# Differential attention in a two-layer decoder trunk: the second run of projection products goes ahead of the output transposes

## The chip, the cores and the metric

The kernel runs on one core of one Trainium2 chip. The metric is the device time of one execution in microseconds (us). Each kernel is timed in several runs, and the median is compared. A single further execution is recorded by the hardware profiler; its times are the ones in the rows below.

## What is computed

The reference is a trunk of two pre-norm layers for 256 tokens of width 1024. Layer 0 mixes tokens with a causal Conformer convolution, layer 1 with causal differential attention. Behind each mixer come a hierarchical mixture of experts and a gated embedding; a final norm ends the trunk. The part that matters here is the attention of layer 1, with 8 heads, two score maps for each head and blocks of 128 queries:

```
qkv = h @ w_qkv                       # (256, 3 * 1024)
q, k = partial_rope(q), partial_rope(k)
for blk in range(2):                  # kend = 128, then 256 keys
    s = einsum("bqhcd,bkhcd->bhcqk", qb, kb) * scale
    a = softmax(where(mask, s, neg))
    wgt = a[:, :, 0] - lam * a[:, :, 1]
    outs.append(einsum("bhqk,bkhd->bqhd", wgt, vb))
o = rms_norm(concat(outs), subln_g) * (1 - lam_init)
return o @ w_o
```

## The kernel before

The order of the instructions on each engine is the order in which the program writes them; every engine works through its own list in that order, and waits in it are resolved by semaphores. Weights stream through a ring of 16 tiles (`wslot`), loaded by SyncE as tiles come free. A product with f32 accuracy is made of three matmuls (L433 to L435): the high halves of both factors, then each low half with the other's high half. So each weight tile is first split: ScalarE writes the high half (L190) and VectorE or, for one of four parts, GpSimd the low half (L191), in `split_part`.

The attention runs over 16 units. Unit n is one head and one block of 128 queries: `units = [(s, hh, qb) for s in range(4) for qb in range(2) for hh in range(2)]`, so four units share a group s of two heads. At n = 4, 8 and 12 `heads(n // 4)` transposes the next group's queries and keys (L1650), and ScalarE evicts them to `qkT` (L1653). Then, in each unit:

- `scores(n)`: score matmuls (L1669); VectorE adds the mask and takes the maximum (L1672, L1675); ScalarE takes the exponentials (L1678).
- `scale_out(n - 2)`: VectorE scales an older unit's output `o` by its norm (L1721).
- `differ(n)`: VectorE combines the two softmax maps into `w` (L1686 to L1690).
- a first pull of 6 products from a generator. In units 0 to 11 this is `projections()`, the products of the queries, keys and values of the next groups, which also issues the splits of later weight tiles (L190, L191), and at a tile's end ScalarE's evictions and VectorE's rotation (L1639 to L1642). In units 12 to 15 it is the output projection (`w_out`), with fewer products for each unit.
- `turn_weights(n - 1)`: transposes of `w` (L1700); ScalarE evicts them to `wT` (L1702).
- `outputs(n - 2)`: the transpose of the scaled `o` (L1727); VectorE multiplies it by the gain into `oT` (L1734). For the last group it is split into two halves, by ScalarE and VectorE.
- a second pull of 6 products.
- `values(n - 1)`: the weights times the values (L1710); ScalarE squares and copies the result (L1714, L1716), GpSimd makes its norm (L390, L391).

The transposes, the weights' transposes, the outputs and the values all take their PSUM tile from one pool of two buffers in turn:

```
def ps_b(name="psb"):
    return psum.tile([P, 512], F32, tag="b", name=name, bufs=2)
```

A unit takes three of them, in the order L1700, L1727, L1710. So the first transposes of `heads` take the buffer that L1727 wrote and L1734 must have read, the second ones that of L1710, and where no `heads` comes between, the next unit's L1700 takes the buffer of L1727.

When the 144 projection products are done, `split_heads` splits the outputs of the first groups (L1746, L1747) and the output projection starts at unit 12. After unit 15 come the routing of the second mixture of experts and its 13 steps (L1157, L1187 and others), whose weights are loaded in part by expert numbers that the routing finds.

Of the kernel before, what the change touches and what calls it, by code (L numbers as in the profile page):

```python
# [91 lines left out]
def kernel(  # L92
# [19 lines left out]
    def ps_b(name="psb"):  # L112
        return psum.tile([P, 512], F32, tag="b", name=name, bufs=2)
# [23 lines left out]
    def channels(row, k):  # L137

        return row.rearrange("p (q c) -> p q c", c=8)[:, :, 4 * k:4 * k + 4]
# [291 lines left out]
    def product(ps, h, c, wh, wl, first, last):  # L431

        nc.tensor.matmul(ps, h[:, 0, c], wh, start=first, stop=False)  # L433
        nc.tensor.matmul(ps, h[:, 0, c], wl, start=False, stop=False)  # L434
        nc.tensor.matmul(ps, h[:, 1, c], wh, start=False, stop=last)  # L435

    def warm(n):

        ps = ps_b("warm") if n else None
        for _ in range(n):  # L440
            nc.tensor.matmul(ps, ones_bf, before[:, None, :].to_broadcast([P, 4, P]), start=True, stop=True)
# [289 lines left out]
    def early(i, n0, n1):  # L731
        if n0 == 0:
            pools[i].open()
        pools[i].load(n0, n1)
# [862 lines left out]
    def attention(ap, R, end):  # L1597
# [46 lines left out]
        def heads(s, half=(0, 1)):  # L1644
            qk = qks[s]
            for hh in half:
                pt = ps_b()
                for n in range(2):
                    for tt in range(2):
                        nc.tensor.transpose(pt[:, n * T + tt * P:n * T + (tt + 1) * P],  # L1650
                                            qk[:, tt, n * 256 + hh * P:n * 256 + (hh + 1) * P], ident)
                qkT = ap.tile([P, 2, T], F32, tag="qkT", name="qkT", bufs=2)
                nc.scalar.activation(qkT.rearrange("p n t -> p (n t)"), pt, AF.Copy)  # L1653
                qkTs[2 * s + hh] = qkT
# [4 lines left out]
        def scores(n):  # L1659
            s, hh, qb = units[n]  # L1660
            qkT = qkTs[2 * s + hh]
            K = (qb + 1) * P
            psc = [ps_e() for _ in range(2)]
            mx = small.tile([P, 2], F32, tag="mx", name="mx", bufs=2)
            z = small.tile([P, 2], F32, tag="z", name="z", bufs=2)
            sc = ap.tile([P, 2, T], F32, tag="sc", name="sc", bufs=2)
            for cc in range(2):
                cs = slice(cc * HD, (cc + 1) * HD)
                nc.tensor.matmul(psc[cc][:, 0:K], qkT[cs, 0, qb * P:(qb + 1) * P], qkT[cs, 1, 0:K],  # L1669
                                 start=True, stop=True)  # L1670
            for cc in range(2):
                nc.vector.tensor_tensor_reduce(sc[:, cc, 0:K], psc[cc][:, 0:K], mask[:, T - K:],  # L1672
                                               1.0, -BIG, op0=ALU.add, op1=ALU.max,
                                               accum_out=mx[:, cc:cc + 1])
            nc.vector.tensor_scalar(mx, mx, -scale, None, op0=ALU.mult)  # L1675
            e = ap.tile([P, 2, T], F32, tag="e", name="e", bufs=2)
            for cc in (1, 0):
                nc.scalar.activation(e[:, cc, 0:K], sc[:, cc, 0:K], AF.Exp, bias=mx[:, cc:cc + 1],  # L1678
                                     scale=scale, accum_out=z[:, cc:cc + 1])
            us[n] = (e, z)  # L1680

        def differ(n):
            s, hh, qb = units[n]
            e, z = us.pop(n)
            K = (qb + 1) * P
            nc.vector.reciprocal(z, z)  # L1686
            nc.vector.tensor_mul(z[:, 1:2], z[:, 1:2], lam)
            nc.vector.tensor_scalar(e[:, 1, 0:K], e[:, 1, 0:K], z[:, 1:2], None, op0=ALU.mult)
            w = ap.tile([P, T], F32, tag="w", name="w", bufs=2)
            nc.vector.scalar_tensor_tensor(w[:, 0:K], e[:, 0, 0:K], z[:, 0:1], e[:, 1, 0:K],  # L1690
                                           op0=ALU.mult, op1=ALU.subtract)
            us[n] = w

        def turn_weights(n):
            s, hh, qb = units[n]
            w = ws[n % 2] = us.pop(n)
            K = (qb + 1) * P
            pw = ps_b()
            for kb in range(qb + 1):
                nc.tensor.transpose(pw[:, kb * P:(kb + 1) * P], w[:, kb * P:(kb + 1) * P], ident)  # L1700
            wT = ap.tile([P, T], F32, tag="wT", name="wT", bufs=2)
            nc.scalar.activation(wT[:, 0:K], pw[:, 0:K], AF.Copy)  # L1702
            us[n] = wT
# [15 lines left out]
        def scale_out(n):  # L1719
            o, ro = us[n]  # L1720
            nc.vector.tensor_scalar(o, o, ro, None, op0=ALU.mult)  # L1721
# [20 lines left out]
        def split_heads(tt, h0, h1):  # L1742
            if tt not in oTs:
                oTs[tt] = work.tile([P, 2, NH, P], F32R, tag="big", name="oTs", bufs=2)
            o = oT[tt][:, h0:h1]
            nc.scalar.activation(oTs[tt][:, 0, h0:h1], o, AF.Copy)  # L1746
            nc.vector.tensor_tensor(oTs[tt][:, 1, h0:h1], o, oTs[tt][:, 0, h0:h1].bitcast(F32), op=ALU.subtract)  # L1747
# [13 lines left out]
        def projections():  # L1761
            for g in atiles[3:]:
                yield from proj(*g)

        def outs():
            for h0, h1 in ((0, 4), (4, 6)):
                for tt in range(2):
                    yield from w_out(tt, h0, h1)
# [5 lines left out]
        def pull(f, n):  # L1774
            for _ in range(n):
                next(f, None)
# [18 lines left out]
        def residual(tt):  # L1795
            for k in range(2):
                add_half(tt, k, wo_ps[tt][k])

        def run():
            f = projections()  # L1800
            heads(0)
            for n in range(16):
                if n == 12:
                    warm(HW[0])
                if n % 4 == 0 and n:
                    heads(n // 4)
                if n == 12:
                    warm(HW[1])
                if n == 12:
                    f = outs()  # L1810
                    if not SH:
                        for tt in range(2):
                            split_heads(tt, 0, 4)
                scores(n)
                if n == 12:
                    warm(HW[2])
                if n >= 2:
                    scale_out(n - 2)
                differ(n)
                quota = QUOTA[n]  # L1820
                pull(f, quota - quota // 2)
                if n >= 1:
                    turn_weights(n - 1)
                if n >= 2:
                    outputs(n - 2)
                pull(f, quota // 2)
                if n == 11:
                    pull(f, 100)
                    if SH == 1:
                        for tt in range(2):  # L1830
                            split_heads(tt, 0, 4)
                if n >= 1:
                    values(n - 1)
                if n == 11 and SH == 2:
                    for tt in range(2):
                        split_heads(tt, 0, 4)
                if n == 13:
                    for tt in range(2):
                        split_heads(tt, 4, 6)
            def last(h):  # L1840
                wh, wl = W.parts(("wo", h // 2))
                for k in range(2):
                    product(wo_ps[1][k], oTs[1], h, channels(wh[:, h % 2], k), channels(wl[:, h % 2], k), False, h == 7)

            scale_out(14)
            pull(w_out(0, 6, 8), 5)
            early(1, 2, 3)
            residual(0)
            turn_weights(15)
            outputs(14)  # L1850
            pull(f, FT[0])
            R.rows(0, 0)
            values(15)
            scale_out(15)
            pull(f, FT[1])
            R.rows(0, 1)
            pull(f, 9)
            if LAST6 == 0:
                last(6)
            outputs(15)  # L1860
            end()
            early(1, 0, 2)
            R.logits(0, 0)
            if LAST6 == 1:
                last(6)
            R.logits(0, 1)
            R.pick(0)
            if LAST6 == 2:
                last(6)
            last(7)  # L1870
            for k in range(2):
                add_half(1, k, wo_ps[1][k])
            R.ranks(0)
            R.spots()
            R.rows(1, 0)
            W.drop(("wo", 3))
# [110 lines left out]
```

## Time and profile before

| what | us |
|---|---|
| median of 3 runs | 797.47 (794.47 to 798.09) |
| the profiled execution | 796.61 |
| its span, first to last instruction | 795.0 |
| TensorE matmul busy | 681.5 (86%) |
| VectorE busy | 385.8 (49%) |
| ScalarE busy | 297.0 (37%) |
| GpSimd busy | 115.8 (15%) |

Times in the rows are counted from the span's start. PE is TensorE's matmul, PEld its weight load, DVE VectorE, ACT ScalarE, POOL GpSimd, SP SyncE. A busy share over the whole span says little, since stages with different limits follow each other: the attention's units lie from 403 to 510 us, the second mixture of experts from 529 to 757 us. A row of a timeline gives start and duration, then the engine, line, instruction, what it writes and reads, its shape and how often it comes in a row; in brackets stands how long the engine was idle before it, and what released it. Matmuls follow each other closer than they last, because they are pipelined.

### The profile page before, as it was taken

The numbers are of one execution on the slowest core, as the hardware profiler recorded it, in microseconds if no ns is written. First come the engines' busy times: TensorE is split into PE (matmuls) and PEld (weight loads), VectorE is DVE, ScalarE is ACT, GpSimd is POOL, SyncE is SP. The second block draws the span as 40 slices with busy tenths as digits, with TensorE's granted clock in tenths as the row PEclk, the third lists the DMA queues.
The fourth block names the chain that finished last, engine by engine and source line by source line (L and its number), as shares of the span: only waits on it lengthen the run. The fifth ranks groups of instructions, "written<-read, shape, count | busy, mean of one in ns | idle before, by whom it ended". The sixth has DMA issues, their size and how long they took to land.

```text
span 795.0 us, 12692 instructions
## 1 busy us (share of the span) xinstructions
PE 681.5 (86%) x4738; PEld 444.3 (56%) x4738; DVE 385.8 (49%) x1022; ACT 297.0 (37%) x668; POOL 115.8 (15%) x191
## 2 busy tenths in 40 slices
PE   5899979889577697679999898988999999876796
PEld 4788757554234242237998696854444455523365
DVE  3599995433032320239677876562443243202174
ACT  1577733521011220018566665542222122210074
POOL 1488730000000000001023432200000000000011
PEclk9899979999899797999999999989999999998899
DMA  6991186799999999999744147857799999999941
GB/s 180 326 409 36 48 323 261 302 420 420 421 420 420 418 418 420 421 385 309 225 159 161 53 152 273 302 231 275 280 406 405 385 420 419 418 421 420 417 165 53
DMA packets 63444, 246.36 MB, mean 310 GB/s; under 512 B 7218, under 2 KB 28403, under 8 KB 43666
## 3 DMA queue, kind: packets, MB, share of 16 engines
q1 hardware_dynamic: 63234, 245.24, 79.3%
q8 instruction: 39, 0.64, 0.3%
q10 hardware_dynamic: 144, 0.26, 0.1%
q14 instruction: 27, 0.22, 0.1%
HBM read 244.43 MB, written 1.05 MB: 309 GB/s over the span
## 4 chain that ended last, share of the span: by engine, by line
PE 28%; DMA 11%; DVE 7%; ACT 6%; issue 1%; POOL 0%; POOLq 0%; ACTq 0%; SPq 0%; DVEq 0%
PE psa L1157 8%; PE psd L1187 4%; DMA wslot<-in_moe_w_up_dram 4%; DMA wslot<-in_moe_w_gate_dram 3%; DMA wslot<-in_moe_w_down_dram 2%; DMA pin<-in_p_dram 2%; PE psb L1089 2%; PE psa L433 2%; DVE wslot L191 2%; PE psa L434 2%; PE psa L435 2%; PE psd L1201 2%; ACT e L1678 1%; ACT wslot L175 1%; PE psc L434 1%
## 5 line engine op out<-in xcount | busy, mean ns | idle before, releaser
L1157 PE MATMUL psa<-wslot,hg 128*32 128x256 f32 (+2 forms) x1712 | 179.8, 474 | 54.7 <-DMA wslot<-in_moe_w_up_dram 29.5
L1157 PEld LDWEIGHTS psa<-wslot,hg 128*32 128x32 f32 (+1 forms) x1712 | 75.9, 128 | 156.0 <-issue 60.4
L1133 DVE TENSOR_REDUCE wc<-psb 32x1 f32<-32x2 f32 (+1 forms) x66 | 10.3, 156 | 197.2 <-PE psb L1128 196.6
L1187 PE MATMUL psd<-wslot,aT 128*32 128x512 f32 (+1 forms) x528 | 78.3, 596 | 6.5 <-ACT aT L1176 1.8
L1164 ACT ACTIVATE sg<-psa 128x256 f32<-128x256 f32 x20 | 7.7, 384 | 188.7 <-PE psa L1157 188.7
L1191 DVE TENSOR_TENSOR dl<-psd,dh 128x512 fp32r<-128x512 f32 x40 | 27.6, 691 | 84.8 <-ACT dh L1190 84.8
L885 PE MATMUL psa<-hT,wslot 128*128 128x256 f32 x256 | 58.6, 388 | 2.5 <-DVE hT L774 2.5
L1204 DVE TENSOR_TENSOR x<-x,psd 128x512 f32<-128x512 f32 x80 | 49.9, 681 | 16.4 <-PE psd L1201 16.4
L885 PEld LDWEIGHTS psa<-hT,wslot 128*128 128x128 f32 x256 | 49.7, 195 | 10.1 <-DVE hT L774 3.0
L1190 ACT ACTIVATE dh<-psd 128x512 fp32r<-128x512 f32 x40 | 23.8, 597 | 72.5 <-PE psd L1187 72.5
L1187 PEld LDWEIGHTS psd<-wslot,aT 128*32 128x32 f32 (+1 forms) x528 | 21.4, 115 | 52.7 <-issue 39.7
L834 DVE SCALAR_TENSOR_TENSOR chain<-vp,wT,chain 128x256 f32<-128x256 f32 x119 | 48.0, 482 | 0.2
L390 POOL TENSOR_SCALAR rstd<-ss 128x1 f32<-128x1 f32 x7 | 3.0, 425 | 292.1 <-ACT sq L397 291.2
L1094 ACT ACTIVATE hg<-psb,gains 128x256 f32<-128x256 f32 x72 | 30.1, 471 | 39.4 <-PE psb L1089 39.4
L433 PE MATMUL psa<-wslot,hTa 128*128 128x256 f32 x144 | 43.6, 302 | 0.0
L1089 PE MATMUL psb<-S,xh 128*128 128x256 f32 x144 | 38.5, 302 | 4.7 <-DVE st L1139 2.0
L434 PE MATMUL psa<-wslot,hTa 128*128 128x256 f32 x144 | 41.3, 287 | 0.0
L435 PE MATMUL psa<-wslot,hTa 128*128 128x256 f32 x144 | 41.3, 287 | 0.0
L809 ACT ACTIVATE prod<-vp,wT 128x256 f32<-128x256 f32 x83 | 35.9, 498 | 12.6 <-POOL vp L799 6.8
L814 POOL TENSOR_TENSOR part<-part,prod 128x256 f32<-128x256 f32 x51 | 35.4, 730 | 0.0
L1089 PE MATMUL psb<-S,xl 128*128 128x256 f32 x144 | 35.3, 279 | 0.0
L191 DVE TENSOR_TENSOR wslot<-wslot 128x512 fp32r<-128x512 f32 x39 | 33.4, 883 | 2.7 <-ACT wslot L190 2.7
(345 smaller groups left out, 1320.2 us busy)
## 6 DMA issues: line engine op xcount, KB each, us to landing
wslot<-in_moe_w_down_dram SPq DMA_DIRECT2D x64, 1024.0 KB
wslot<-in_moe_w_gate_dram SPq DMA_DIRECT2D x44, 1024.0 KB
wslot<-in_moe_w_up_dram SPq DMA_DIRECT2D x44, 1024.0 KB
wslot<-in_moe_w_gate_dram SPq DMA_DIRECT2D x34, 512.0 KB
wslot<-in_moe_w_up_dram SPq DMA_DIRECT2D x34, 512.0 KB
wslot<-in_conv_w_pw_dram SPq DMA_DIRECT2D x12, 1024.0 KB
wslot<-in_da_w_qkv_dram SPq DMA_DIRECT2D x12, 1024.0 KB
wslot<-in_ple_w_gate_dram SPq DMA_DIRECT2D x8, 1024.0 KB
```

Of the source, the lines that this page charges most:

```text
L191: eng.tensor_tensor(lo, w, hi.bitcast(F32), op=ALU.subtract)
L433: nc.tensor.matmul(ps, h[:, 0, c], wh, start=first, stop=False)
L434: nc.tensor.matmul(ps, h[:, 0, c], wl, start=False, stop=False)
L435: nc.tensor.matmul(ps, h[:, 1, c], wh, start=False, stop=last)
L809: nc.scalar.activation(pr, vps[j][:, k:k + T], AF.Copy, scale=wT[:, j, k:k + 1])
L814: nc.gpsimd.tensor_tensor(part[:, n % 2], part[:, n % 2], pr, op=ALU.add)
L834: nc.vector.scalar_tensor_tensor(pc[n], vps[j][:, k:k + T], wT[:, j, k:k + 1], pe if start else pc[n], op0=ALU.mult, op1=ALU.add)
L885: nc.tensor.matmul(pws[j][:, (1 - half) * T:(2 - half) * T], W.get("pw1", j // 2, 1 - half)[:, c, j % 2 * P:(j % 2 + 1) * P], hT[:, c], st ...
L1089: nc.tensor.matmul(ps[:, c * 256:(c + 1) * 256], xx[tt][:, cc], S[:, tt], start=(n == 0), stop=(n == 3))
L1157: nc.tensor.matmul(out, hg[:, c, s1:s1 + width], w, start=(c == 0), stop=(c == 7))
L1187: nc.tensor.matmul(pd[at:at + w], aT[:, c, at:at + w], W.get("down", i, e)[:, c, k * 512:(k + 1) * 512], start=(c == 0), stop=(c == 1))
L1204: nc.vector.tensor_add(x[:, tt, ks], x[:, tt, ks], ps)
```

## The change

The second pull moves from behind `outputs(n - 2)` to in front of it, in all 16 units.

```
                 if n >= 1:
                     turn_weights(n - 1)
+                pull(f, quota // 2)
                 if n >= 2:
                     outputs(n - 2)
-                pull(f, quota // 2)
                 if n == 11:
                     pull(f, 100)
```

TensorE, unit 7 into unit 8, before: the transposes of the weights (`w`), that of the older output (`o`), then the 18 matmuls of the second pull, of which the first three stand here.

```order
L1700 MATMUL psb<-ident,w 128x128 x2
L1727 MATMUL psb<-ident,o 128x128
L433 MATMUL psa<-wslot,hTa 128x256
L434 MATMUL psa<-wslot,hTa 128x256
L435 MATMUL psa<-wslot,hTa 128x256
```

The same place now, from the last two matmuls of the second pull to the next group's head transposes (`qk`) and scores:

```order
L434 MATMUL psa<-wslot,hTa 128x256
L435 MATMUL psa<-wslot,hTa 128x256
L1727 MATMUL psb<-ident,o 128x128
L1710 MATMUL psb<-v,wT 128x128 x2
L1650 MATMUL psb<-ident,qk 128x128 x8
L1669 MATMUL pse<-qkT 128x128 x2
```

L1727 stands right ahead of L1710 and three places ahead of the scores, and the 18 matmuls follow L1700 directly.

VectorE, unit 7 into unit 8 (`w` is the end of `differ`, L191 the low halves of weight tiles, `oT` the copy out of PSUM, `sc` the scores of unit 8):

```order
 L1688 TENSOR_SCALAR e<-e,z 128x256
 L1690 SCALAR_TENSOR_TENSOR w<-e,z 128x256
-L191 TENSOR_TENSOR wslot<-wslot 128x512
-L1734 TENSOR_SCALAR oT<-psb,subln 128x128
-L191 TENSOR_TENSOR wslot<-wslot 128x512 x3
+L191 TENSOR_TENSOR wslot<-wslot 128x512 x4
+L1734 TENSOR_SCALAR oT<-psb,subln 128x128
 L1672 ISA sc,mx<-pse,mask 128x128
 L1672 ISA mx 128x1
```

The copy has moved behind three low halves and is the last thing ahead of the next unit's scores.

VectorE, unit 3 into unit 4, with the same names:

```order
 L1688 TENSOR_SCALAR e<-e,z 128x256
 L1690 SCALAR_TENSOR_TENSOR w<-e,z 128x256
-L1734 TENSOR_SCALAR oT<-psb,subln 128x128
 L191 TENSOR_TENSOR wslot<-wslot 128x512 x2
+L1734 TENSOR_SCALAR oT<-psb,subln 128x128
 L1672 ISA sc,mx<-pse,mask 128x128
 L1672 ISA mx 128x1
```

Here it has moved behind two. Unit 11 goes from two low halves, the copy and one more to three and the copy. The orders of ScalarE, GpSimd and SyncE are the same in both kernels.

## Rows read from the trace of the kernel before

**Rows 1.** Busy us (count) of PE, PEld, DVE, ACT, POOL; clock; DMA share; GB/s.
```profile
403.00:486.00 83.00, 73.67 (x569) 66.82 (x567) 65.76 (x201) 55.18 (x167) 28.73 (x34) 0.98 0.40 143
486.00:516.00 30.00, 30.00 (x162) 24.25 (x162) 15.25 (x63) 14.37 (x49) 5.72 (x19) 1.00 0.77 272
535.00:575.00 40.00, 36.70 (x194) 17.93 (x193) 13.50 (x50) 11.93 (x33) 0.00 (x0) 1.00 0.74 264
575.00:757.00 182.00, 159.32 (x1225) 79.77 (x1228) 51.80 (x112) 34.65 (x75) 0.00 (x0) 0.96 1.01 412
```

**Rows 2.** Chain that ended last, of the attention's units 0 to 11, by line.
```profile
by line: DVE wslot L191 19.3%; ACT e L1678 9.2%; issue 7.3%; ACT wslot L190 6.8%; DVE sc L1672 6.5%; PE psa L433 5.7%; PE psa L435 4.9%; PE psa L434 4.9%; DVE r L1639 4.2%; DVE qk L1642 3.7%; PE pse L1669 2.9%; DVE oT L1734 2.4%; PE psb L16
```

**Rows 3.** TensorE's waits, units 0 to 11: us in total, times, longest us.
```profile
PE psb L1727 <- DVE o L1721: 4.8, 5, 1.8
PE psb L1650 <- DVE oT L1734: 2.5, 3, 1.2
```

**Rows 4.** VectorE's waits in the same stretch.
```profile
DVE z L1686 <- ACT e L1678: 10.4, 12, 1.0
```

**Rows 5.** TensorE's timeline, unit 7 into 8: start, us, instruction, idle before.
```profile
448.77 0.38 PE L1700 MATMUL psb<-ident,w 128*128 128x128 f32 x2
450.97 0.33 PE L1727 MATMUL psb<-ident,o 128*128 128x128 f32 x1 [1.81 <-DVE o L1721]
453.28 0.69 PE L1710 MATMUL psb<-v,wT 128*128 128x128 f32 x4
455.20 1.21 PE L1650 MATMUL psb<-ident,qk 128*128 128x128 f32 x8 [1.23 <-DVE oT L1734]
456.55 0.49 PE L1669 MATMUL pse<-qkT 64*128 64x128 f32 x4
```

**Rows 6.** VectorE's timeline, unit 7 into 8.
```profile
449.75 0.41 DVE L1672 CUSTOM_DVE_ANT_0 sc<-pse,mask 128x256 f32<-128x256 f32 x1
453.12 1.76 DVE L191 TENSOR_TENSOR wslot<-wslot 128x512 fp32r<-128x512 f32 x1
454.81 0.34 DVE L1734 TENSOR_SCALAR oT<-psb,subln 128x128 f32<-128x128 f32 x1
455.07 2.95 DVE L191 TENSOR_TENSOR wslot<-wslot 128x512 fp32r<-128x512 f32 x3
457.94 0.28 DVE L1672 CUSTOM_DVE_ANT_0 sc<-pse,mask 128x128 f32<-128x128 f32 x1
```

**Rows 7.** ScalarE's timeline, unit 7: eviction of the weights' transposes.
```profile
452.85 0.36 ACT L1702 ACTIVATE wT<-psb 128x256 f32<-128x256 f32 x1
```

**Rows 8.** VectorE's timeline, unit 3 into 4.
```profile
426.58 0.34 DVE L1734 TENSOR_SCALAR oT<-psb,subln 128x128 f32<-128x128 f32 x1
426.85 1.28 DVE L191 TENSOR_TENSOR wslot<-wslot 128x512 fp32r<-128x512 f32 x2
428.84 0.29 DVE L1672 CUSTOM_DVE_ANT_0 sc<-pse,mask 128x128 f32<-128x128 f32 x1 [0.72 <-PE pse L1669]
```

**Rows 9.** VectorE's timeline, end of unit 4.
```profile
433.12 1.97 DVE L191 TENSOR_TENSOR wslot<-wslot 128x512 fp32r<-128x512 f32 x2 [0.35 <-ACT wslot L190]
435.00 0.28 DVE L1672 CUSTOM_DVE_ANT_0 sc<-pse,mask 128x128 f32<-128x128 f32 x1
```

**Rows 10.** VectorE's timeline, unit 11 into 12.
```profile
483.22 0.34 DVE L1734 TENSOR_SCALAR oT<-psb,subln 128x128 f32<-128x128 f32 x1
483.48 1.56 DVE L191 TENSOR_TENSOR wslot<-wslot 128x512 fp32r<-128x512 f32 x1
```

**Rows 11.** TensorE's and ScalarE's timelines, unit 11 into 12.
```profile
485.38 0.66 PE L1650 MATMUL psb<-ident,qk 128*128 128x128 f32 x4 [1.11 <-ACT o L1716]
485.21 0.61 ACT L1653 ACTIVATE qkT<-psb 128x512 f32<-128x512 f32 x1
```

**Rows 12.** Busy time of two stretches of unit 8's products (columns as rows 1).
```profile
457.20:460.40 3.20, 3.20 (x16) 3.20 (x16) 2.25 (x12) 1.66 (x7) 1.15 (x2) 0.50 0.02 5
461.00:463.20 2.20, 2.20 (x20) 2.20 (x19) 1.91 (x4) 1.94 (x4) 0.00 (x0) 1.00 0.00 0
```

More of the change, by code (lines that the diff above doesn't have):

```diff
@@ L1823, in run @@
                     turn_weights(n - 1)
+                pull(f, quota // 2)
                 if n >= 2:
                     outputs(n - 2)
-                pull(f, quota // 2)
                 if n == 11:
```

## The prediction

> **What bounds the kernel now.** I read the stretches first [rows 1]. From 575 to 757 us the 16 DMA engines are busy all the time (share 1.01, 412 GB/s): that stage lasts as long as its bytes take, and only its start can move. Its start hangs on what came before, since from 535 to 575 the DMA share is 0.74: the loads wait there for tiles that TensorE frees, so what the attention gives or loses is handed on. From 486 to 516 TensorE is busy 30.00 of 30 us with the output projection and never waits, so it also hands on whatever the attention ends with. The change acts in front of that, in units 0 to 11 (403 to 486 us). There TensorE is busy 73.67 of 83 us, VectorE only 65.76, ScalarE 55.18, and still TensorE is not what sets the pace: the chain that ended last is led by VectorE's L191 (the low halves of the weights, 19.3%), then ScalarE's exponentials (L1678, 9.2%) and L190 [rows 2]. VectorE's idle time is mostly the 12 waits for those exponentials, 10.4 us [rows 4], a round trip inside each unit (scores, maximum, exponential, back). That time is not slack, because VectorE runs in order and its next work stands behind it. So in most units VectorE and the round trip form a closed loop, and TensorE runs ahead of it and waits.
>
> TensorE's waits in units 0 to 11 are of two kinds that matter here [rows 3]: 4.8 us for a scaled output (L1727 on L1721, five times), and 2.5 us at the head transposes (L1650 on L1734, three times, once for each new group of heads). The second kind is a wait for a buffer: the first head transposes take the psb buffer that the transposed output of outputs(n - 2) leaves, and VectorE must have copied that out (L1734).
>
> **The change, part by part.** No instruction is added or removed, and ScalarE, GpSimd and SyncE keep their order. On TensorE the 18 products of the second pull (9 in units 12 to 15, or 6) now run before the transpose L1727 and not behind it. On VectorE the copy L1734 falls behind the low halves (and rotations) which that pull issues.
>
> *First, the stall that goes.* In unit 7 TensorE stands 1.81 us in front of L1727 [rows 5]. With the products ahead of it, o is ready when they end. But what follows is values(n - 1), and this needs wT from ScalarE, whose place behind that unit's exponentials is unchanged: in unit 7 L1702 runs from 452.85 to 453.21 [rows 7], and L1710 already starts at 453.28 [rows 5]. The stall moves by 18 products and ends at the same moment, so there is nothing to gain in that unit. In the other four cases a few tenths of TensorE's time come free, and then TensorE meets VectorE at the next boundary. I take 0; the bounds are 0 and −4.8 us, all five waits.
>
> *Second, a buffer that comes free later inside a unit.* L1700 of unit 7 takes the buffer of the older output whose copy now stands last ahead of that unit's scores, so it can start at about 449.75, when the scores' L1672 starts [rows 6], and not at 448.77 [rows 5]. That is a new wait of 1.0 us. It lies under the wait for wT up to 453.21 as long as 449.75 plus the transposes and the products (451.05 to 453.28 before, 2.23) comes to about 452.2. Cost 0, at most 1.0 if that cover goes.
>
> *Third, the boundaries of the groups of heads (units 3 to 4, 7 to 8, 11 to 12).* Here heads() follows at once and wants the buffer of L1734. The work in the block stays the same, so the copy now ends where the block's last L191 ended.
> Unit 3 to 4: from 426.58 + 0.34 = 426.92 to 426.85 + 1.28 = 428.13, +1.21 us [rows 8]. Scores of unit 4 follow the head transposes and their eviction, VectorE is already waiting for them (0.72 us before 428.84), and so both engines shift by 1.21.
> Unit 7 to 8: from 454.81 + 0.34 = 455.15 to 455.07 + 2.95 = 458.02, three low halves later, +2.87 us [rows 6]. The head transposes move from 455.20 to 458.1 and unit 8's score products from 456.55 [rows 5] to 459.4. VectorE used to start unit 8's scores at 457.94, without a wait, so its own shift is about 2.0; TensorE's is 2.87. Unit 8 was bound by TensorE, whose products ran there at 1.2 GHz (granted clock 0.50 [rows 12]). I take 2.87. If the slow stretch happened to fall on the longer idle time, 16 products at 3.20/16 = 0.20 us would take 2.20/20 = 0.11 us, 1.4 us would come back, and 1.4 would be left.
> Unit 11 to 12: from 483.22 + 0.34 = 483.56 to 483.48 + 1.56 = 485.04, +1.48 us [rows 10]. Much of that was lost already, since the second half of the transposes waited 1.11 us for ScalarE, until 485.38, and the first eviction began only at 485.21 [rows 11]. By unit 8's spacing (455.20 to 456.55) scores come 1.35 after the first transpose, at 485.10 + 1.35 = 486.45; before, the second half's start at 485.38 plus its 0.66, with an overlap, let them begin at about 486.0. +0.5 us.
>
> *Fourth, unit 4.* There VectorE had a gap in front of 433.12 (0.35 us, for ScalarE's high halves) and the copy lay beside it; afterwards L191 runs up to 435.00, where the next scores start at once [rows 9]. The copy now stands behind it and adds its spacing, 455.07 − 454.81 = 0.26 us [rows 6]. In units 5, 6, 9 and 10 it only changes places within a block that was busy throughout: 0.
>
> In units 12 to 15 TensorE never waits and VectorE is half idle (15.25 of 30 us [rows 1]), so the later copies cost nothing; if a split of the last heads came late, the price would be one copy, 0.3 us.
>
> The sum is 1.21 + 0.26 + 2.87 + 0.5 − 0 = 4.84 us. The profiled execution took 796.61 us (span 795.0 and 1.6 around it); 796.61 + 4.84 = 801.45, and as the median of the runs lies 0.86 above that execution, 802.3 us.
>
> **The rivals.** *Gain.* TensorE has the highest occupancy, and its 4.8 us at L1727 could come off: 797.47 − 4.8 = 792.7 us. For it speaks that units 4 and 5 and the first half of unit 8 run without a TensorE wait. It decides if heads() does not stand behind the later copy, that is if VectorE gets through its low halves before TensorE is done with values; at unit 7 it is 4 us late. Against it stand rows 2 and 7. The Trainium skill, "Perfetto Trace Analysis", section "Identifying the Most-Contended Engine", says to take the engine with the highest occupancy as the bottleneck and to optimize it first, and that for TensorE the weight loads' share is the better measure; by either measure here (73.67 or 66.82 of 83) that is TensorE, and by that rule the change gives the 4.8 us. 8 in 100.
>
> *Absorbed.* The shift at 3 to 4 stays at 1.2, that at 7 to 8 falls to 1.4 because the slow stretch meets idle time, and one of the others is taken up: 1.2 + 1.4 = 2.6 us, 800.1 us. For it: VectorE's shift at unit 8 is smaller than TensorE's. 20 in 100.
>
> *More slow clock.* The granted clock fell to 0.50 from 457.2 to 460.4 [rows 12], after two waits of 1.81 and 1.23 us [rows 5]. The waits at L1650 grow to about 2.3 us (unit 4), 4.1 (unit 8) and 2.2 (unit 12), so it may fall at unit 4 or 12 too, or stay low longer in unit 8. Each such stretch costs 16 × (0.20 − 0.11) = 1.4 us where TensorE sets the pace; two of them give 797.47 + 4.84 + 2.8 = 805.1 us. The Trainium skill, "TensorE: Matmul & The Clock Gate", section "A second HAM failure mode: psum-queue depth-cycling", says that a kernel which cycles PSUM buffers with many short idle times loses throughput as the clock falls and rises again; the trace agrees for unit 8 (0.50 in rows 12), and no run here shows it for units 4 and 12. 12 in 100.
>
> **How the numbers follow.** The forecast holds 60 in 100, of which some 14 lie below +4.0 us. That is 0.5% of 797.47, about what a measurement of this kernel can tell from no change. Slower by over 0.5%: 46 + 12 = 58. Within 0.5%: 14 + 20 + 1 (a small gain) = 35. Faster: 7. The range goes from 799.0 (below it lie the gain and a part of the absorbed case) to 806.5 (two slow stretches and another microsecond), which leaves out about 18 in 100.
>
> **What the changed profile would show.** The wait L1727 on L1721 nearly gone (under 1 us); L1650 on L1734 grown from 2.5 to about 8.6 us in three waits, the longest about 4 us at unit 8; the wait on L1716 at unit 12 gone; new waits of about 1 us each at L1710 on ScalarE's wT and at L1700 on L1734 in units 7 and 11. The four low halves of unit 7 in one row, with the copy behind them. The first products of the output projection at about 491 us, and not at 486.4; the DMA-bound stage as long as before and as much later. I am wrong if that start moves by under 3 us, if L1650 waits for something else, or if the stage after 575 us takes up the shift.

## The result

The changed kernel is slower: 802.06 us in the median of 9 runs (798.1 to 804.25), against 796.21 us for the kernel before, run beside it (9 runs, 794.44 to 798.09). The ratio is 1.0072, with a 95% interval of 1.0054 to 1.009. The forecast was 802.3 us, slower by 4.84 us. The direction, the place and the time were right; what the loss is made of was not, as the traces show.

The profiled execution of the changed kernel has a span of 802.6 us. TensorE's waits in units 0 to 11, to set against [rows 3] (us in total, times, longest us):

```profile
PE psb L1650 <- DVE oT L1734: 4.7, 3, 2.2
PE psb L1710 <- ACT wT L1702: 4.5, 3, 1.9
PE psb L1650 <- ACT o L1716: 1.8, 1, 1.8
```

The wait at L1727 (4.8 us before) is gone. In its place TensorE waits 4.5 us for `wT` ahead of the values. At the head transposes it now waits 4.7 us for the copy L1734 (2.5 before) and 1.8 us for ScalarE's copy L1716. TensorE's timeline from unit 7 into unit 8, to set against [rows 5]:

```profile
458.23 0.71 PE L1710 MATMUL psb<-v,wT 128*128 128x128 f32 x4 [1.87 <-ACT wT L1702]
460.72 1.11 PE L1650 MATMUL psb<-ident,qk 128*128 128x128 f32 x4 [1.78 <-ACT o L1716]
463.07 1.12 PE L1650 MATMUL psb<-ident,qk 128*128 128x128 f32 x4 [1.23 <-DVE oT L1734]
464.11 0.80 PE L1669 MATMUL pse<-qkT 64*128 64x128 f32 x4
```

The wait of 1.81 us at L1727 has become one of 1.87 us at L1710, and the head transposes, which came 1.92 us after the values before (453.28 to 455.20), now come 2.49 and 4.84 us after them. VectorE at the same place, to set against [rows 6]:

```profile
458.09 4.66 DVE L191 TENSOR_TENSOR wslot<-wslot 128x512 fp32r<-128x512 f32 x4
462.67 0.34 DVE L1734 TENSOR_SCALAR oT<-psb,subln 128x128 f32<-128x128 f32 x1
464.94 0.29 DVE L1672 CUSTOM_DVE_ANT_0 sc<-pse,mask 128x128 f32<-128x128 f32 x1 [1.93 <-PE pse L1669]
```

All four low halves now stand ahead of the copy, and VectorE, which started unit 8's scores without a wait before, waits 1.93 us for them.

What the prediction did not put into its sum stands in the granted clock. Busy us (count) of PE, PEld, DVE, ACT and POOL, clock, DMA share and GB/s, for units 0 to 11 and for three stretches at units 4, 8 and 12:

```profile
404.00:494.00 90.00, 78.34 (x571) 70.57 (x571) 66.19 (x202) 55.71 (x168) 29.03 (x34) 0.90 0.40 141
...
428.30:435.60 7.30, 6.28 (x29) 5.72 (x30) 3.40 (x14) 3.32 (x9) 1.03 (x2) 0.54 0.42 144
459.20:466.20 7.00, 4.25 (x18) 3.29 (x19) 4.69 (x11) 3.11 (x11) 2.75 (x4) 0.53 0.00 0
490.30:497.20 6.90, 5.58 (x18) 4.08 (x19) 4.64 (x15) 4.46 (x14) 3.08 (x3) 0.51 1.00 373
```

TensorE ran at 1.2 GHz for some 7 us at each of the three boundaries; before, units 0 to 11 had one such stretch, of 3.2 us [rows 12]. The slow matmuls are busy for longer, so TensorE's busy time rises from 73.67 to 78.34 us with the same work.

VectorE's timeline at the end of unit 4 shows how this becomes a loss. Before, it waited 0.35 us there for ScalarE's high halves [rows 9]:

```profile
437.81 1.98 DVE L191 TENSOR_TENSOR wslot<-wslot 128x512 fp32r<-128x512 f32 x2 [2.11 <-ACT wslot L190]
```

ScalarE in turn had stood 1.38 us in front of the eviction L1702, for the weights' transposes (L1700) that TensorE runs behind its slow products.

To see where the shift arises, I take the start of VectorE's first mask instruction (L1672) in a unit, counted from the first head transpose of unit 0 (402.48 us before, 403.64 after), and subtract the value of before:

| start of | after, us later |
|---|---|
| scores of units 0 to 3 | 0.0 |
| scores of unit 4 | 2.05 |
| scores of units 5, 6, 7 | 3.81, 3.81, 3.80 |
| scores of units 8, 9 | 5.84, 5.94 |
| scores of units 11, 12 | 6.20, 6.96 |
| scores of unit 13 | 8.18 |
| first matmul of the mixture of experts (L1157) | 8.10 |
| end of the span | 6.44 |

The loss arises at the three boundaries and in the unit behind each of them; outside these only 0.26 us comes in unit 10. The last line says less than it seems to: from the first L1157 to the end the profiled execution of before took 266.1 us, that of the changed kernel 264.5, and those of the eleven kernels below 262 to 265 us, whatever came ahead. The stage bound by the DMA engines is as long as it was (its share is 1.01 from 580 to 763 us) and starts later. A single execution's shift is not the median's either: runs of the kernel before differ by 3.7 us.

### The profile page after: what moved, and what is told of

It reads as the page before. It is cut to its first block, busy times and chain, and to the rows that moved or that the text cites. A ratio compares the mean times of both kernels' runs of the same rounds, so it can differ in the third digit from the quotient of the medians.

```text
span 802.6 us, 12695 instructions
## 1 busy us (share of the span) xinstructions
PE 692.9 (86%) x4738; PEld 451.2 (56%) x4738; DVE 386.2 (48%) x1022; ACT 297.6 (37%) x668; POOL 115.5 (14%) x191
## 4 chain that ended last, share of the span: by engine, by line
DMA 35%; PE 33%; DVE 18%; ACT 9%; issue 2%; POOL 1%; SPq 1%; POOLq 0%; ACTq 0%; DVEq 0%
DMA wslot<-in_moe_w_up_dram 12%; DMA wslot<-in_moe_w_down_dram 9%; PE psa L1157 9%; DMA wslot<-in_moe_w_gate_dram 7%; DVE chain L834 5%; PE psd L1187 4%; DVE wslot L191 3%; PE psb L1089 3%; DMA pin<-in_p_dram 2%; DMA wslot<-in_ple_w_gate_dram 2%; PE psd L1027 2%; PE psd L1201 2%; ACT wslot L175 2%; PE psa L433 2%; DMA wslot<-in_conv_w_pw_dram 1%
## 5 line engine op out<-in xcount | busy, mean ns | idle before, releaser
L1157 PE MATMUL psa<-wslot,hg 128*32 128x256 f32 (+2 forms) x1712 | 180.6, 478 | 49.9 <-DMA wslot<-in_moe_w_up_dram 27.3
L1157 PEld LDWEIGHTS psa<-wslot,hg 128*32 128x32 f32 (+1 forms) x1712 | 76.1, 129 | 151.8 <-issue 60.9
L885 PE MATMUL psa<-hT,wslot 128*128 128x256 f32 x256 | 61.1, 399 | 3.0 <-DVE hT L774 3.0
L885 PEld LDWEIGHTS psa<-hT,wslot 128*128 128x128 f32 x256 | 51.5, 202 | 11.3 <-DVE hT L774 3.5
L191 DVE TENSOR_TENSOR wslot<-wslot 128x512 fp32r<-128x512 f32 x39 | 32.4, 868 | 4.8 <-ACT wslot L190 4.8
```

The source lines that it names most:

```text
L191: eng.tensor_tensor(lo, w, hi.bitcast(F32), op=ALU.subtract)
L885: nc.tensor.matmul(pws[j][:, (1 - half) * T:(2 - half) * T], W.get("pw1", j // 2, 1 - half)[:, c, j % 2 * P:(j % 2 + 1) * P], hT[:, c], st ...
L1157: nc.tensor.matmul(out, hg[:, c, s1:s1 + width], w, start=(c == 0), stop=(c == 7))
```

## The theories and the experiments

Theory A is the prediction's mechanism: the copy L1734 behind the low halves keeps a psb buffer from the next heads at three places. Its rival B puts the loss on the later copy and on the bunched psb tiles in every unit. A second question came from the trace: theory C says that most of the loss is TensorE's clock, which falls in the waits; theory D that the waits alone make it, as the prediction's sum has it. Each ratio below is against the kernel before, run on the same chip.

**The three boundary units alone, and all units but these.** In the kernel before, the place of the second pull is made to depend on n:

```
+                if n in (3, 7, 11):
+                    pull(f, quota // 2)
                 if n >= 2:
                     outputs(n - 2)
-                pull(f, quota // 2)
+                if not (n in (3, 7, 11)):
+                    pull(f, quota // 2)
```

> The second pull stands ahead of the output transposes only in units 3, 7 and 11, the last ones before a new group's head transposes; in the other 13 units the order is that of before. Theory A (the copy L1734 behind the low halves keeps a psb buffer from the head transposes at three places, and TensorE's clock falls in those waits): the whole loss is here, ratio 1.005 to 1.009, L1650 waits on L1734 for 4 us or more in total. Theory B (the loss comes from the later copy and the bunched psb tiles in every unit): these are 3 of 16 units, ratio at most 1.002.

Measured: 803.3 us, ratio 1.0089 (1.0066 to 1.0113).

> The opposite: the new order in all units but 3, 7 and 11. Theory A: nothing is left of the loss, ratio 0.998 to 1.002, L1650 waits on L1734 for about 2.5 us as before, and the wait at L1727 (4.8 us before) is small because only units 3, 7 and 11 keep it (3.9 us of the 4.8 lie there). Theory B: 13 of 16 units keep the change, ratio 1.005 or more.

Measured: 795.69 us, ratio 0.9996 (0.9984 to 1.0009), with `not in` in place of `in`. The three units carry the whole loss, and the change in the other 13 is worth nothing that can be measured. Theory B falls. In only_bound L1650 waits 4.7 us for L1734, as A had it. In not_bound the wait at L1727 is 4.1 us, near the expected 3.9, and L1650 waits 1.3 us for L1734, where 2.5 was expected:

```profile
PE psb L1727 <- DVE o L1721: 4.1, 3, 1.8
PE psb L1710 <- ACT wT L1702: 1.8, 2, 0.9
PE psb L1650 <- ACT o L1716: 1.3, 2, 1.1
PE psb L1650 <- DVE oT L1734: 1.3, 2, 0.8
```

**Another buffer for the output transposes.** For the outputs of units 0 to 9, `outputs` takes its tile from another pool of PSUM buffers, the c pool, which stands idle there:

```
-            pot = ps_b()
+            pot = ps_c() if n < 10 else ps_b()
```

> The changed kernel, with the output transposes of units 0 to 9 in a PSUM tile of the c pool, which is free in units 2 to 11; the order of every engine is that of the changed kernel, so the copy L1734 is as late, but nothing of the next heads waits for it. Theory A: the loss goes, ratio 0.997 to 1.002, no wait of L1650 on L1734, and the second half of the head transposes waits at most for ScalarE's copy o. Theory B: the order is unchanged and so is the loss, ratio 1.005 to 1.009.

Measured, with the changed order: 797.25 us, ratio 1.0015 (1.0001 to 1.0029).

> The kernel before, with the output transposes of units 0 to 9 in the c pool. It takes away the 2.5 us in which L1650 waited for L1734 and leaves the 4.8 us at L1727. Theory A: what TensorE gains at unit 8 is mostly given to ScalarE's copy o, which ends about 0.5 us later than L1734 did there, so a gain of 0.3 to 1.0 us, ratio 0.9985 to 1.000. Theory B says the same; the run is the partner of the third one, and the difference of the two is what the order alone is worth once the buffer is out of the way.

Measured, with the order of before: 795.77 us, ratio 0.9992 (0.9978 to 1.0007). With the changed order kept, the other buffer alone takes the loss from 0.72% to 0.15%. VectorE's timeline of after_pc, unit 3 into unit 4, shows the copy as late as in the changed kernel, and unit 4's scores right behind it:

```profile
427.27 1.28 DVE L191 TENSOR_TENSOR wslot<-wslot 128x512 fp32r<-128x512 f32 x2
428.48 0.34 DVE L1734 TENSOR_SCALAR oT<-psc,subln 128x128 f32<-128x128 f32 x1
428.74 0.27 DVE L1672 CUSTOM_DVE_ANT_0 sc<-pse,mask 128x128 f32<-128x128 f32 x1
```

So it is the buffer, and not the late copy by itself. The 0.15% that is left goes with two slow stretches at units 8 and 12, after the waits for `wT` and for ScalarE's `o` (clock 0.54 and 0.57 in windows about them):

```profile
455.00:462.50 7.50, 6.61 (x30) 6.06 (x31) 5.62 (x16) 4.13 (x14) 2.66 (x3) 0.54 0.01 2
486.00:494.00 8.00, 7.02 (x23) 5.35 (x24) 3.61 (x12) 3.28 (x11) 1.90 (x3) 0.57 0.80 304
```

**The clock: idle matmuls in the waits of the changed kernel.** A helper issues matmuls whose result nothing reads, where TensorE would wait:

```
+        def busy(n):
+            ps = ps_c("busy") if n else None
+            for _ in range(n):
+                nc.tensor.matmul(ps, ones_bf, before[:, None, :].to_broadcast([P, 4, P]), start=True, stop=True)
...
                 if n % 4 == 0 and n:
+                    busy(HEADS_AT[n])        # {4: 9, 8: 12, 12: 6}
                     heads(n // 4)
...
+                busy(VALUES_AT.get(n, 0))    # {7: 8, 11: 8}
                 if n >= 1:
                     values(n - 1)
```

> The changed kernel, with idle matmuls (bf16, 512 columns, a PSUM tile of the c pool that nothing reads) where TensorE waits: 8 ahead of the values in units 7 and 11, and 9, 12 and 6 ahead of the head transposes of units 4, 8 and 12. By 0.22 us each they fill 1.8, 2.0, 2.6 and 1.3 us of waits of 1.9, 2.2, 3.0 and 1.4 us. Theory C (a good part of the loss is TensorE's clock, which falls in all three waits): the granted clock stays at 1.00 from 403 to 497 us, and the loss falls to the waits alone, 1.21 + 0.26 + 1.4 + 0.5 = 3.4 us, ratio 1.003 to 1.005. Theory D (the waits alone make the loss, as the prediction's sum has it, and the clock is worth what it was worth before): ratio 1.006 to 1.009.

Measured: 797.04 us, ratio 1.0007 (0.9993 to 1.0021). The order, the buffers and the late copies are those of the changed kernel, and the loss is gone but for 0.07%. The clock of units 0 to 11:

```profile
404.00:495.00 91.00, 87.10 (x644) 74.40 (x644) 69.39 (x216) 57.49 (x174) 29.20 (x34) 1.00 0.44 159
```

With the waits filled the clock stays at 2.4 GHz. Unit 4's scores come 1.20 us later than before (2.05 in the changed kernel), unit 5's 1.46 (3.81), unit 9's 2.09 (5.94), and the output projection starts 2.37 us later (6.96). The copy is as late as it was, and at unit 4 the boundary costs with the full clock what the prediction took for its wait (1.20 against 1.21 us). Theory D falls, and C is right in kind: 0.65 of the 0.72% come back. C's own figure of 1.003 to 1.005 was missed; it left out that the slow stretch of before goes as well. That part is not the order's: it is measured below, in before_warm.

**The boundaries one by one.** The new order in a single unit:

> The new order in unit 3 alone. Prediction's sum: 1.21 + 0.26 = 1.5 us, ratio 1.0019. With a slow stretch of TensorE in unit 4, as in the trace of the changed kernel (shift of unit 5's scores 3.8 us): ratio 1.0048.

Measured: 796.89 us, ratio 1.001 (0.9997 to 1.0022).

> The new order in unit 7 alone. Prediction's sum: 2.87 us, ratio 1.0036. By the trace of the changed kernel, where unit 9's scores shift by 5.9 - 3.8 = 2.1 us: ratio 1.0027.

Measured: 798.4 us, ratio 1.0018 (1.0004 to 1.0033).

> The new order in unit 11 alone. Prediction's sum: 0.5 us, ratio 1.0006. By the trace of the changed kernel, where unit 12's scores shift by 1.0 us more and the output projection starts at 1.2 GHz: 1.0 to 2.0 us, ratio 1.0012 to 1.0025.

Measured: 796.69 us, ratio 1.0008 (0.9994 to 1.0021). Only3 stays under both of its expected figures, only7 is nearer to the lower of its two, only11 to the prediction's. The three add up to 0.36%, under half of what they cost together in only_bound (0.89%). The traces show a reason: in the profiled execution of only3 the clock did not fall at all. TensorE there has the same wait of 2.16 us at the same place. The waits and head transposes of the changed kernel, of only_bound, then of only3:

```profile
429.32 1.97 PE L1650 MATMUL psb<-ident,qk 128*128 128x128 f32 x8 [2.16 <-DVE oT L1734]
```

```profile
428.83 1.97 PE L1650 MATMUL psb<-ident,qk 128*128 128x128 f32 x8 [2.16 <-DVE oT L1734]
```

```profile
429.27 1.09 PE L1650 MATMUL psb<-ident,qk 128*128 128x128 f32 x8 [2.16 <-DVE oT L1734]
```

And what only3 did in the stretch that stands above for the changed kernel with 29 matmuls and a clock of 0.54:

```profile
428.30:435.60 7.30, 6.08 (x50) 5.73 (x51) 3.90 (x16) 4.74 (x13) 1.64 (x3) 1.00 0.44 144
```

Fifty matmuls in place of 29. In only3 unit 4's scores come 1.19 us late and unit 5's 1.20, with nothing more. Even the slow stretch of before in unit 8 is missing, though TensorE waits there as before (1.82 and 1.23 us against 1.81 and 1.23): unit 9's scores come 0.08 us earlier than before. VectorE at unit 3 into 4:

```profile
427.67 1.28 DVE L191 TENSOR_TENSOR wslot<-wslot 128x512 fp32r<-128x512 f32 x2
428.87 0.34 DVE L1734 TENSOR_SCALAR oT<-psb,subln 128x128 f32<-128x128 f32 x1
431.13 0.29 DVE L1672 CUSTOM_DVE_ANT_0 sc<-pse,mask 128x128 f32<-128x128 f32 x1 [1.92 <-PE pse L1669]
```

In the changed kernel the slow clock adds 3.81 − 1.20 − 0.26 = 2.35 us to that by unit 5: its low halves then wait the 2.11 us shown above. In only7 the shift is 2.07 us at unit 8 and 3.34 at unit 9, behind a slow stretch from 453 to 463 us. In only11 unit 12's scores do not come later at all (−0.30, where unit 11's were at −0.50), and the slow products behind them cost 1.33 us more by unit 13. The length of a wait alone thus does not decide whether the clock falls, and a median of several runs can hold both cases. The mean granted clock over the whole execution, which is on record for every timed run, bears this out: it averages 0.940 in the 35 runs of the kernel before, 0.941, 0.939 and 0.939 in only3, only7 and only11 (12 each), but 0.932 in only_bound (6), 0.934 in the changed kernel (9) and 0.946 in after_warm (12). The single boundaries hardly cost clock; the three together do.

**Both remedies.** Idle matmuls in the waits of three more kernels, with `heads` written in two halves so that some can stand between them. First the kernel before:

> The kernel before, with idle matmuls where TensorE waits in units 6, 7 and 11 (3, 8 and 7 ahead of the output transposes) and at the heads of units 8 and 12 (5 and 3 ahead of the first half, 5 ahead of the second at unit 12). Theory C (the clock carries most of the loss): the slow stretch of unit 8, worth 1.3 us by the run with unit 3 alone, goes, and any that falls in unit 12: ratio 0.996 to 0.999. Theory D (the clock is a small matter): ratio 0.999 to 1.001.

Measured: 794.62 us, ratio 0.9986 (0.9974 to 0.9997).

> The kernel before with the output transposes of units 0 to 9 in the c pool, and idle matmuls in the waits left: 3, 8 and 7 ahead of the output transposes of units 6, 7 and 11, 1 and 9 between the halves of the head transposes of units 8 and 12. Without them this kernel had two slow stretches of about 3.4 us. Theory C: 0.6 us of the free buffer and 1.3 to 2.6 us of clock, ratio 0.995 to 0.998, faster than both kernels. Theory D: as without the idle matmuls, 0.999 to 1.000.

Measured: 793.76 us, ratio 0.9966 (0.9952 to 0.998).

> The changed order with the output transposes of units 0 to 9 in the c pool, and idle matmuls in the waits left: 3, 8 and 8 ahead of the values of units 6, 7 and 11, 6 and 9 between the halves of the head transposes of units 8 and 12. With buffer and clock out of the way this shows what the order itself is worth: theory C, the same as the partner with the old order, ratio 0.995 to 0.999, within 0.1% of it; theory D, as without the idle matmuls, 1.001 to 1.002.

Measured: 793.66 us, ratio 0.9974 (0.9963 to 0.9986). Both are faster than either kernel, and all three ratios lie where theory C put them. Their clock is 1.00 from 403 to 490 us; for the last one:

```profile
403.00:490.00 87.00, 83.54 (x626) 72.17 (x625) 68.50 (x212) 56.79 (x173) 29.35 (x34) 1.00 0.48 164
```

All ratios side by side show what the order costs in each setting:

| | order of before | changed order | difference |
|---|---|---|---|
| as written | 1 | 1.0072 | 0.0072 |
| output transposes in the c pool | 0.9992 | 1.0015 | 0.0023 |
| idle matmuls in the waits | 0.9986 | 1.0007 | 0.0021 |
| both | 0.9966 | 0.9974 | 0.0008 |

The row of the idle matmuls gives the clock's share: with the waits filled in both orders the order costs 0.21%, so 0.51 of the 0.72% is clock, and the other 0.14 of the 0.65 that came back in after_warm is the slow stretch that the kernel before has too. Either remedy takes away two thirds of the loss, and with both the order makes no difference that these intervals can tell.

## Why the prediction was right, and where it was not

**The bound.** Right between the boundaries. VectorE and its round trip with ScalarE set the pace: shifts arise at a boundary and then stand unchanged over units (3.81, 3.81, 3.80), and the chain that ended last is again led by L191 (25.0% of units 0 to 11). At the boundaries VectorE waits for TensorE: its waits for the scores rise from 2.8 to 6.5 us. The stage bound by the DMA engines took nothing back.

**The stall that goes: 0.** Right. It moved to L1710, and unit 7's 1.81 us became 1.87. The prediction gave the other four waits a few tenths of a microsecond, but that of unit 11 was 1.57 us before:

```profile
479.86 0.33 PE L1727 MATMUL psb<-ident,o 128*128 128x128 f32 x1 [1.57 <-DVE o L1721]
```

It moved in the same way, to 1.89 us at L1710. The new order outside the boundaries, where the remaining 0.9 us of stalls lie, is worth nothing (not_bound). The gain of the first rival did not come.

**The buffer that comes free later inside a unit.** The cost of 0 was right, the mechanism wrong. No wait of L1700 for L1734 appears: in the changed kernel L1700 of unit 7 starts ahead of the copy that it was to wait for.

```profile
453.72 0.38 PE L1700 MATMUL psb<-ident,w 128*128 128x128 f32 x2
454.45 0.34 DVE L1734 TENSOR_SCALAR oT<-psb,subln 128x128 f32<-128x128 f32 x1
```

So the pool does not always hand out its two buffers in turn, as the description before the prediction says. At unit 8 too the first half of the head transposes waits for ScalarE's `o` and only the second for L1734. The buffer of the late copy had gone to the second half.

**Unit 3 to 4: +1.21, and unit 4: +0.26.** Right within 0.02 us with the clock full: 1.19 in only3 and 1.20 in after_warm, 1.46 behind unit 4 in after_warm, and 0.26 at unit 5 in not_bound. The same 0.26 us arises in unit 10 too (5.94 to 6.20 in the changed kernel, the same step in not_bound), which I had put at 0. But the changed kernel lost 3.81 us here.

**Unit 7 to 8: +2.87, 1.4 without a slow stretch.** The term mixed a wait with the clock. With the clock full, unit 8's shift was 1.28 us above unit 7's (1.44 to 2.72 in after_warm), and unit 9's only 0.65 above, since before has its slow products there and after_warm has none. The changed kernel lost 2.14 us up to unit 9 (3.80 to 5.94); alone, with a long slow stretch, it was 3.34 us (only7).

**Unit 11 to 12: +0.5.** Too much where the clock was still full (0.0 in after_warm, 0.2 in only11) and too little without: 0.76 us at unit 12's scores and 1.22 more by unit 13, where the output projection starts at 1.2 GHz.

**The step that failed** is the clock, whose change the sum put at nothing. The sum left it as it had been and made more slow clock a rival with 12 in 100, at 1.4 us for a stretch of 3.2 us as in [rows 12]. In the profiled execution the clock fell at all three boundaries and stayed low for about 7 us each time. By unit 13 the changed kernel is 8.18 us late and after_warm 2.4, so a full clock gives back 5.8 us there; in the timed runs it is 1.0072 against 1.0007, or 5.2 of 5.7 us. Some 1.1 us of this the kernel before loses to the clock as well (before_warm, 0.9986); what the change adds by the clock is about 4.1 us (0.51%), and by the waits 1.7 us (0.21%). The sum of 4.84 us came close to the measured 5.85 us by luck: it counted TensorE's slow products in unit 8 in full and put too much on units 8 and 12, while it left out most of the clock's price, and the errors largely cancelled. That the time was met within 0.3 us is luck too, since the forecast stood on 797.47 us for the kernel before, which took 796.21 beside the changed one. The Trainium skill ("TensorE: Matmul & The Clock Gate", "A second HAM failure mode: psum-queue depth-cycling") warns of short idle times at PSUM buffers by which the clock falls and rises again. The traces agree, with clocks of 0.54, 0.53 and 0.51 at the three boundaries, and I had weighed it too low.

The signs that the prediction named: the wait at L1727 gone (right); L1650 on L1734 grown to 8.6 us with one wait of 4 us (4.7 us, the longest 2.2, because part of it shows as waits for `wT` and `o`); the wait on L1716 gone from unit 12 (right, but there is one of 1.78 us at unit 8, so that L1650 did wait for something else, which the prediction had named as a sign of being wrong); new waits at L1710 (right in place, 4.5 us in all, more than the 1 us each that I had named); the output projection at about 491 us (494.51, of which 1.16 lie ahead of the attention).

Two things stay open. What makes the clock fall after one wait of 2.16 us and not after another was not tried. And the median's loss (5.85 us) is smaller than the shift in the profiled executions (8.10 us at L1157). The mean clocks point to why: the profiled execution of before had 0.946, above the 0.940 of its timed runs, and that of the changed kernel 0.931, below its 0.934. In which units the clock fell in the timed runs is not on record.

## What to carry to other kernels

When a step is moved behind other work, look up what its result frees: here a copy of 0.34 us held a PSUM buffer that the next group's transposes needed, and VectorE, which works in the order written, first ran four low halves (4.66 us in unit 7) that now stand ahead of it. Price a new wait on TensorE twice, once by its length and once at half clock for the matmuls behind it; here the second was the larger part. And if such a wait can't be avoided, matmuls that nothing reads in its place are a cheap trial: they took away most of this loss, and with a spare PSUM buffer made both orders faster than the kernel before.

## What I had not expected of the hardware

The granted clock fell at a wait of 2.16 us in two kernels (the changed one and only_bound) and not in a third with the same wait (only3), whose order up to there is that of only_bound. Once it fell it stayed at 1.2 GHz for about 7 us although TensorE was busy for 6.28 of 7.30 us in that time, where in the kernel before such a stretch was 3.2 us long.
